# Casting the weights by DMA once per tile pair, without a bf16 copy in HBM, and a new order of work at the pair's seam

## The chip, the cores and the metric

The kernel runs on all 8 NeuronCores of one Trainium2 chip, each core on its own eighth of the tokens, with no exchange between cores. The metric is the device time of the slowest core, in microseconds (us); lower is better. The program has two states: in some executions the cores of one die, or of both, get a lower TensorE clock and the time is up to 19% longer. Such runs are called slow, and their times are left out; every comparison of times below is between fast runs. Chips also differ a little: the fast runs of the kernel before take 3500 to 3507 us on some of the chips used here and 3477 to 3482 us on others (one of them 3507), so ratios are always taken against runs of the kernel before on the same chip. The record shows where this difference is: on the slower chips, some pairs of cores have a mean clock of 0.98 in each run and take 3490 to 3506 us, while the cores at 0.99 take 3463 to 3479 us. On the other chips nearly all cores are at 0.99.

Where a profile is read, it is that of the slowest core unless another is named, because that core sets the metric.

## The reference, cut to what matters

One decoder layer over 32 x 2048 tokens, model width 1024. All sizes are those of the reference.

```python
# h   = x + RMSNorm(MixerBlock(RMSNorm(x)))
# out = h + RMSNorm(SwiGLU(RMSNorm(h)))
proj = xn @ w_in                        # 1024 -> 3840: q 512 | k 128 | v 128 | u 512 | v' 512 | gate_a 1024 | gate_b 1024
attn = banded_sink_attention(q, k, v)   # 8 heads, window 128, ALiBi, sinks
gm   = gelu(u) * (W_s LN(gelu(v')) + b) # causal 128 x 128 mixing in each chunk
merged = sigmoid(gate_a) * (attn @ w_attn_branch) + sigmoid(gate_b) * (gm @ w_gmlp_branch)
mix  = merged @ w_out
ff   = (silu(hn @ w_gate) * (hn @ w_up)) @ w_down   # 1024 -> 2816 -> 1024
```

A core has 8192 tokens: 16 tiles of 512 tokens, worked on as 8 pairs (tile A and tile B). Weights are float32 in HBM and bf16 on the chip. They are cut into 31 chunks of at most 1 MB (bf16), which stream through a ring of five buffers: `C_Q`, `C_KV`, `C_U`, `C_VG` (projections), eight `M` chunks (gates and branch projections, "merge"), two `O` (output projection), eleven `G` (gate and up) and six `D` (down). PSUM has 8 banks of 128 x 512 float32.

## The kernel before

In the kernel before, a chunk is read as float32 by a casting DMA (from GpSimd's queue) for its first few uses (one to five). It is then saved as bf16 to HBM (`wbf`) and read back from there by plain DMAs (SyncE's queue). The `M`, `O` and `D` chunks, and those of Q and KV, are streamed twice per pair, once for each tile.

```python
    def stream_init(self):
        ...                                   # M, O, G, DN: lists of chunks
        for s in range(npair):
            order += M + O + M + O + G + DN
            if s + 1 < npair:
                order += [C_Q, C_KV]
            order += DN
            if s + 1 < npair:
                order += [C_U, C_VG, C_Q, C_KV]

    def record_load(self):
        ...
        if c in self.saved:                   # bf16 copy exists: plain load
            self.dma(self.W(s, 0, ln), AP(self.wbf_d, ...), [("wbf", c)], wkey, ("W", s))
            return
        self.dma(self.W(s, 0, ln), AP(self.wsrc_d, ...), [], wkey, ("WC", s), q="pool", ...)   # cast load
        if k >= SAVE_AT[c] and c in self.order[n + 1:]:
            self.to_save.add(n)
```

Down works on one tile at a time with four PSUM banks; the projections and the attention of the next pair's tile A are laid inside the down of tile B, and x of the next tile B is loaded early in it (`k == 3`):

```python
            self.down(tA, 0)
            ...
            self.front_a(tA + 2, 0)           # Q and KV of the next tile A
            att = self.attn(tA + 2, 0)

            def hook_d(k):                    # called after each of 24 blocks of matmuls
                if k % 2 == 0:
                    next(att, None)           # a step of attention
                if k == 3:
                    self.load_x(tB + 2)
                if k in (17, 19, 21, 23):
                    bx.append(self.rms(tB + 2, (k - 17) // 2))   # normalise a 128-token block

            self.down(tB, 1, hook_d)
            ...
            self.proj_u(su, 0)
            self.tr_x(bx, 1)                  # transposes of the next tile B
            self.proj_vg(sv, 0)
            ...
```

At the start, constants are loaded and prepared before the first projection; one of the preparations is a matmul:

```python
        self.load_x(0)
        self.load_consts(0)
        self.release(0)                       # five weight loads at once
        self.load_x(1)
        self.tr_x([self.rms(0, b, ...) for b in range(NB)], 0)
        self.load_consts(1)                   # holds: self.mm(P(bk), ones, wsT, ...), needs all constants
        sq = self.acquire(C_Q)
        self.proj_q(sq, 0)
```

The softmax here doesn't subtract the row's maximum and nothing guards it: scores larger than these inputs give would overflow.

## Time and profile before

| what | value |
|---|---|
| time, median of the fast runs | 3504.9 us (fast runs 3504.12 to 3504.91, one slow run 3674.33) |
| share of TensorE busy | 95% |
| one pair of tiles, settled | 419.9 us, of which TensorE idle 9 |
| to the start of the first down | 453.2 us |
| from the start of the seventh pair's down to the end | 507.0 us |

These are lines of the profile page of the kernel before. First comes the busy time of each engine (its share, and the number of instructions). Then follow the busy share of TensorE and its granted clock in 40 equal slices, the two DMA queues (packets, MB, share of 16 engines) and the chain of waits that ended last.

```profile
PE 3332.8 (95%) x17497; PEld 1561.3 (45%) x17497; DVE 1257.0 (36%) x1817; ACT 863.0 (25%) x1199; POOL 508.6 (15%) x592
PE   2899989999999999999999999999999999999998
PEclk9888999999999999999999999999999999999999
...
q1 hardware_dynamic: 70560, 393.85, 32.7%
q0 software_dynamic: 19200, 64.75, 12.3%
...
PE 92%; DVE 3%; DMA 3%; issue 1%; POOL 1%; ACT 1%; SPq 0%; DVEq 0%; POOLq 0%; ACTq 0%
```

TensorE bounds this kernel. The row of slices shows one weak place, the start; after it there are nines, but for an 8 in the sixth slice and in the last.

The chain in order of time shows the settled period. These two lines of it (start, duration) are the transposes of the next tile A just before down, in pairs 4 and 5:

```profile
1734.32 1.79 PE ps L538 x32
...
2154.52 1.79 PE ps L538 x32
```

They are 420.2 us apart, and down begins as the transposes end (in the first pair at 451.42 + 1.79 = 453.2 us). TensorE's waits between them (in total, number, longest) are short ones:

```profile
PE ps L365 <- DVE X L371: 2.9, 1, 2.9
PE ps L365 <- DVE tmp L374: 2.8, 3, 1.1
PE ps L365 <- POOL R L371: 2.6, 2, 1.4
PE ps L365 <- DVE R L385: 0.6, 3, 0.2
PE ps L365 <- ACT tmp L368: 0.2, 1, 0.2
```

Their sum is 9.1 us. The engines' busy time in the same stretch (then clock, DMA share, GB/s) gives TensorE's work:

```profile
1734.30:2154.50 420.20, 410.88 (x2186) 193.46 (x2184) 155.92 (x225) 107.07 (x149) 56.76 (x64) 1.00 0.38 128
```

So 411 us per pair is what the matmuls take, at full clock, and a reordering can win at most 9 us there. The rest of the loss is at the edges, and the start is the largest part. This is the timeline around the first projection:

```profile
57.00 0.69 DVE L371 TENSOR_TENSOR wsT<-tmp 128x512 bf16<-128x512 f32 x1 [11.49 <-DMA g4bc<-c_g4bc]
...
57.84 0.58 PE L365 MATMUL ps<-wsT,ones 128*128 128x512 bf16 x1 [14.35 <-DVE wsT L371]
...
58.22 2.34 PE L365 MATMUL ps<-X,ring 128*128 128x512 bf16 x5
```

The first projection begins at 58.2 us. The bracket is the idle time of the engine before the instruction and what ended it.

On this core the clock is also low from 140 to 310 us: 0.81. These are the busy times of that stretch, as above, of this core and of core 5:

```profile
140.00:310.00 170.00, 166.09 (x745) 71.84 (x745) 74.01 (x101) 46.30 (x60) 52.81 (x60) 0.81 0.84 145
140.00:310.00 170.00, 161.93 (x861) 76.01 (x862) 79.35 (x107) 49.56 (x63) 54.09 (x62) 0.99 0.85 158
```

Core 5 starts 116 matmuls more; at 0.216 us each they make about 25 us. The starts of the first down agree: 423.0 us on core 4 and 426.0 on core 5, and 452 to 453 on the other six. So the low clock costs 27 to 30 us here.

### The profile page before, as it was taken

The page shows a single profiled execution, that of the slowest core. Times are in us where ns is not written, and L with a number is a line of the kernel's source. Part 1 is how long each engine was busy: PE and PEld are TensorE (multiplying, and loading weights), DVE is VectorE, ACT ScalarE, POOL GpSimd, SP SyncE. Part 2 cuts the span into 40 slices and gives each one's busy share as a digit, 9 for nine tenths or more (in the row PEclk, how much of TensorE's full clock was granted, in tenths as well). Part 3 has the DMA queues.
Part 4 walks back from the last instruction along what each step waited for, and adds up shares of the span by engine and source line. Part 5 has one row for each costly group of instructions (what it writes and reads, how often), then busy time and mean ns, then how long its engine had stood idle before and what let it go on. Part 6 is the DMA issues. An engine that isn't in the chain of part 4 may idle for free.

```text
span 3505.0 us, 46677 instructions; the slowest of 8 cores (3464.7 to 3505.0 us)
## 1 busy us (share of the span) xinstructions
PE 3332.8 (95%) x17497; PEld 1561.3 (45%) x17497; DVE 1257.0 (36%) x1817; ACT 863.0 (25%) x1199; POOL 508.6 (15%) x592
## 2 busy tenths in 40 slices
PE   2899989999999999999999999999999999999998
PEld 1444434444444444444444444444444444444443
DVE  2433125431254313542245411453125531254312
ACT  2222113321132212331132311332113321132211
POOL 1131101310012100120001300122001210012100
PEclk9888999999999999999999999999999999999999
DMA  6487688842755225432264322543235422534223
GB/s 169 67 137 154 141 164 190 162 130 83 172 184 165 85 81 190 151 133 84 82 204 139 129 83 86 187 149 120 86 129 170 145 98 82 173 123 142 84 82 135
DMA packets 89980, 461.60 MB, mean 132 GB/s; under 512 B 9632, under 2 KB 9760, under 8 KB 64032
## 3 DMA queue, kind: packets, MB, share of 16 engines
q1 hardware_dynamic: 70560, 393.85, 32.7%
q0 software_dynamic: 19200, 64.75, 12.3%
q8 instruction: 145, 2.38, 0.3%
q14 instruction: 75, 0.61, 0.1%
HBM read 460.41 MB, written 62.91 MB: 149 GB/s over the span
## 4 chain that ended last, share of the span: by engine, by line
PE 92%; DVE 3%; DMA 3%; issue 1%; POOL 1%; ACT 1%; SPq 0%; DVEq 0%; POOLq 0%; ACTq 0%
PE ps L365 90%; PE ps L538 2%; DVE tmp L374 1%; DMA tmp<-c_ident 1%; DMA wbf<-ring 1%; POOL R L371 1%; DVE X L371 1%; DMA g4bc<-c_g4bc 0%; DMA ring<-wsrc 0%; PE ps L690 0%; ACT PT L368 0%; SPq L389 0%; DVE R L385 0%; ACT tmp L368 0%; DVE xb L374 0%
## 5 line engine op out<-in xcount | busy, mean ns | idle before, releaser
L365 PE MATMUL ps<-X,ring 128*128 128x512 bf16 x8832 | 1964.7, 383 | 32.4 <-DVE X L371 23.3
L365 PEld LDWEIGHTS ps<-X,ring 128*128 128x128 bf16 x8832 | 864.5, 99 | 1081.3 <-issue 106.1
L368 ACT ACTIVATE tmp<-ps 128x1024 f32<-128x1024 f32 (+1 forms) x528 | 485.5, 921 | 2036.1 <-PE ps L365 1966.6
L365 PE MATMUL ps<-ring,R 128*128 128x512 bf16 x3840 | 859.7, 383 | 23.3 <-POOL R L371 19.8
L365 PEld LDWEIGHTS ps<-ring,R 128*128 128x128 bf16 x3840 | 372.1, 99 | 479.5 <-issue 69.7
L371 DVE TENSOR_TENSOR R<-ps,tmp 128x1024 bf16<-128x1024 f32 x176 | 215.6, 1225 | 960.9 <-PE ps L365 937.8
L371 POOL TENSOR_TENSOR stats<-stats,neghalf 128x1 f32<-128x1 f32 (+2 forms) x240 | 144.6, 602 | 1950.3 <-DVE stats L381 1710.8
L374 DVE SCALAR_TENSOR_TENSOR tmp<-tmp,ps 128x1024 f32<-128x1024 f32 x128 | 156.2, 1220 | 324.1 <-PE ps L365 315.3
L365 PE MATMUL ps<-R,ring 128*128 128x512 bf16 x1024 | 247.9, 386 | 0.0
L371 POOL TENSOR_TENSOR R<-tmp 128x512 bf16<-128x512 f32 x128 | 166.4, 1300 | 497.4 <-DVE tmp L374 465.5
L368 ACT ACTIVATE PT<-ps 128x1024 bf16<-128x1024 f32 x124 | 126.7, 1024 | 245.1 <-PE ps L365 232.7
L374 DVE SCALAR_TENSOR_TENSOR xb<-tmp,stats,xb 128x1024 f32<-128x1024 f32 x128 | 160.3, 1283 | 67.2 <-POOL stats L371 59.3
L371 DVE TENSOR_TENSOR tmp<-ps,g4bc 128x512 f32<-128x512 f32 x128 | 84.5, 688 | 268.5 <-ACT tmp L368 158.4
L365 PEld LDWEIGHTS ps<-R,ring 128*128 128x128 bf16 x1024 | 99.5, 99 | 124.8 <-issue 23.1
L371 DVE TENSOR_TENSOR X<-ps,g 128x1024 bf16<-128x1024 bf16 x128 | 150.3, 1216 | 8.8 <-PE ps L538 8.8
L371 DVE TENSOR_TENSOR PT<-PT,tbl 128x1024 bf16<-128x1024 bf16 x124 | 95.5, 771 | 151.1 <-ACT PT L368 150.3
L368 ACT ACTIVATE xn<-xb 128x1024 bf16<-128x1024 f32 x128 | 133.9, 1049 | 44.7 <-DVE stats L381 36.9
L365 PE MATMUL ps<-ring,X 128*128 128x512 bf16 (+1 forms) x1024 | 144.3, 299 | 0.0
L381 POOL TENSOR_SCALAR xn<-xb,stats 128x1024 bf16<-128x1024 f32 x124 | 138.7, 1119 | 29.7 <-POOL stats L371 25.7
L391 POOL DMA_DIRECT2D ring<-wsrc x72 | 52.9, 735 | 509.8 <-PE ps L365 416.2
L538 PE MATMUL ps<-ident,xn 128*128 128x128 bf16 x1024 | 70.2, 223 | 39.4 <-DVE stats L381 37.2
L365 PEld LDWEIGHTS ps<-ring,X 128*128 128x128 bf16 x1024 | 79.7, 98 | 62.3
(46 smaller groups left out, 897.8 us busy)
## 6 DMA issues: line engine op xcount, KB each, us to landing
ring<-wbf SPq DMA_DIRECT2D x181, 1024.0 KB, 5.0
ring<-wbf SPq DMA_DIRECT2D x125, 768.0 KB, 4.8
ring<-wsrc POOLq DMA_DIRECT2D x34, 1024.0 KB, 10.8
xb<-x SPq DMA_DIRECT2D x64, 512.0 KB, 9.4
y<-xb SPq DMA_DIRECT2D x64, 512.0 KB, 4.4
ring<-wsrc POOLq DMA_DIRECT2D x35, 768.0 KB, 10.4
wbf<-ring SPq DMA_DIRECT2D x20, 1024.0 KB, 9.2
wbf<-ring SPq DMA_DIRECT2D x10, 768.0 KB, 9.1
```

What stands on the lines that cost most here:

```text
L365: self.op("pe", lambda e: e.matmul(out, lhsT, rhs, start=start, stop=stop), reads, writes)
L368: self.op("act", lambda e: e.activation(out=out, in_=in_, func=func, **kw), reads, writes)
L371: self.op(eng, lambda e: e.tensor_tensor(out=out, in0=a, in1=b, op=alu), reads, writes)
L374: self.op("dve", lambda e: e.scalar_tensor_tensor(out=out, in0=a, scalar=sc, in1=b, op0=op0, op1=op1), reads, writes)
L381: fn = lambda e: e.tensor_scalar(out=out, in0=a, scalar1=s1, scalar2=s2, op0=op0, op1=op1)
L391: fn = lambda e: e.dma_start(out=out, in_=in_, max_dma_last_dim=max_last)
L538: self.op("pe", lambda e, o=o, x=x: e.transpose(out=o, in_=x, identity=idn), [("xn", i), ("c", "ident")], [("ps", bk)])
```

## The change

The intent: each chunk is loaded once per pair by a casting DMA, used for tile A and tile B while it is in the ring, and freed. That removes the bf16 copy and its saves, and leaves 248 weight loads in place of 390. The bytes read from HBM do not fall, since all of them are now float32. To use a down chunk for both tiles at once, down needs all 8 PSUM banks. So nothing else can run inside it, and the attention of tile A moves from down to the Q and U projections of tile B; that of tile B moves to the first merge steps. The diff, cut to its core:

```diff
     def stream_init(self):
-        ...
-        for s in range(npair):
-            order += M + O + M + O + G + DN
-            ...
+        self.order = list(range(NCH)) * (self.n_tiles // 2)

     def record_load(self, after=()):
-        if c in self.saved:
-            self.dma(self.W(s, 0, ln), AP(self.wbf_d, ...))
-            return
         self.dma(self.W(s, 0, ln), AP(self.wsrc_d, ...), list(after), [("ring", s)], ("WC", s), q="pool", ...)

-    def down(self, t, par, hook=None):
+    def down(self, tA, tB):
         for hf in range(2):
             for ci, nk in enumerate((8, 8, 6)):
                 slot = self.acquire(C_D0 + 3 * hf + ci)
+                for par in range(2):
                     for b in range(NB):
+                        bk = 4 * par + b                   # all 8 banks
                         ...
+                        if ci == 2:
+                            self.down_evac(tiles[par], par, b, hf, bk, tys[b], tj)

+    def down_evac(self, t, par, b, hf, bk, ty, tj):
+        self.act(..., AF.Square, ..., accum_out=...)       # ScalarE: sum of squares
+        self.tt("dve", yh[hf], self.P(bk), g, ALU.mult)    # VectorE: times the norm's gain
+        if hf == 0:
+            return
+        self.tt("dve", ...)                                # the two half sums
+        self.norm_stats((s, 1), EPS, rk)                   # VectorE, then GpSimd's power -1/2
+        self.stt(...)                                      # VectorE: x += y * r, waits for GpSimd
+        self.store_y(t, b)

+    def front(self, tA, tB, mid_consts=False):
+        ...                                                # Q, KV, U of A; blocks 0, 1 of B normalised
+        self.proj_vg(sv, 0, lambda h: hv(1) if h == 0 else None)   # blocks 2, 3 normalised
+        for b in range(NB):
+            self.tr_block(bx[b], 1, b, self.g1, "g1")      # transposes of B after VG of A
+        att = self.attn(tA, 0)
+        self.proj_q(sq, 1, step2)                          # Q of B, with attention of A in it
+        self.proj_u(su, 1, lambda: next(att, None))
+        ...                                                # KV of B, spatial of A, VG of B

     def record(self):
         self.load_x(0)
         self.load_consts(0)
-        self.release(0)
-        self.load_x(1)
+        self.record_load()
+        self.record_load([("xb", 0, 1)])                   # further weight loads wait for x
+        for _ in range(NSLOT - 2):
+            self.record_load([("xb", 0, 3)])
+        self.load_x(1, [("ring", 0)])
         ...
-            self.down(tA, 0)
-            self.front_a(tA + 2, 0)
-            self.down(tB, 1, hook_d)
+            self.down(tA, tB)
+            if nxt:
+                self.load_x(tB + 2)                        # x of the next B: after down
+                self.front(tA + 2, tB + 2)
```

In the same diff, merge steps of A and B alternate, and the matmul of constants moves behind the first projections (`load_consts(3)`).

## The prediction

> **What bounds it now.** TensorE: busy 95% on the page, 92% of the chain of waits that ended last. In the settled state (that chain in order of time) a pair of tiles takes 419.9 us (1734.3 to 2154.3), of which TensorE waits only 9.1 (X transposes 2.9, tmp 2.8, merged R from POOL 2.6). 608 gate/up matmuls take 131.4 us, 216 ns each. So 411 us per pair is the floor. The rest of the loss is at the edges: TensorE works 6 of the first 60 us (DMA share about 1.0; the identity landed after 29 us), the first pair reaches its last transposes at 451 us where matmuls alone need about 335, the second pair takes 444 (waits on the wbf save and weight DMAs, 15 and 27 us), the tail is 12.
>
> **What the change does.**
> - DMA: the wbf round trip goes; all 248 loads become cast loads from POOL. 64.75 MB in 12.3% of 3505 us is 150 GB/s landed, so 29.4 MB per pair takes about 196 us of 440: not a bound. A 1 MB chunk takes 7 us and feeds 13.8 us of matmuls. The Trainium skill ("DMA: Bandwidth & Descriptors", SWDGE vs HWDGE vs iDMA) says casts must be issued from GpSimd; the trace agrees (all casts are in the software queue).
> - Start: one chunk, not five, competes with the first x. Projections start at about 27 us (58 before), those last transposes come at 360 to 395, depending on whether the clock is again 0.81 from 140 to 310 us. Worth 55 to 90 us. The second pair's extra 24 us go; the tail gains 4.
> - Merge: A and B alternate, so the R waits (2.6) and the wait at gate/up (2.9) go.
> - Front, added: (a) Down's last evacuation is eight in-order VectorE blocks: 0.69 multiply, 0.26 add, 1.08 scalar to power and back, 1.22 update: 3.2 us each, while TensorE fills a bank every 1.3 us. VectorE is 17 us behind when down ends. U's first half needs bank 7, freed at +14.7, wanted at +10.4: 4 us idle. (b) x for tile B is loaded after the last of those stores; its transposes follow VG directly, with Q of B right behind. Their evacuations (4 x 1.16) queue on VectorE behind both VG tails (5.4 us each) and two normalisations. I get Q of B at +45 instead of +26. Total about 19 us idle per front. (c) Restart is cold: the Trainium skill ("TensorE: Matmul & The Clock Gate", The HAM clock gate) halves the clock after about 3.4 us idle; here 32 matmuls took 8.97 us at 92 us, not 6.9. Plus 2. (d) Denser attention: 3 to 4 us for A, 4 to 5 for B (3.6 now).
>
> **Sum.** Per pair 411 + 19 + 2 + 4 + 4, less slack: 438, against 420; seven fronts lose about 125 us. First part 379, six periods 2628, last 542: 3550 us.
>
> **What the profile should show.** TensorE busy and granted clock drop once per pair, just after down; the longest TensorE waits are on X by VectorE (about 10 us, 7 times) and tmp by VectorE (about 4). If instead Q of B starts by +30, I am wrong there and the time is near 3400. Software DMA 45 to 50% of the span, no TensorE wait on ring over 3 us in the settled state.
>
> **What would make it wrong.** VectorE chains shorter than summed; the start throttled differently; cast loads issued late by POOL's queue (closest at out-projection: 12 us in hand against about 13): slower.

## The result, and the profile after

The changed kernel takes 3612.8 us (median of four fast runs, 3609.53 to 3616.18), against 3504.9 before. The ratio is 1.0309, with a 95% interval of 1.0288 to 1.0329. A ratio here is taken over the fast runs of both kernels in the same rounds, so it is not quite the ratio of the medians that are quoted. The change makes the kernel 3.1% slower.

These are the same lines of the page as above, for the changed kernel:

```profile
PE 3325.3 (92%) x17497; PEld 1557.9 (43%) x17497; DVE 1291.2 (36%) x1977; ACT 875.2 (24%) x1206; POOL 607.8 (17%) x784
PE   4999979999799997999979999799997999979997
PEclk9999989999899998999989999899998999999999
...
q0 software_dynamic: 66432, 234.90, 39.4%
q1 hardware_dynamic: 20160, 70.08, 5.4%
...
PE 76%; DVE 9%; issue 6%; DMA 4%; POOL 2%; ACT 2%; DVEq 0%; SPq 0%; POOLq 0%; ACTq 0%
```

The start is better (the first slice is 4, not 2), but a 7 comes once per pair, and the clock dips in the same slices. On the chain that ended last, VectorE has gone from 3% to 9%. The two lines of the chain that answer to those of before are the transposes of the next tile A in pairs 4 and 5:

```profile
1716.18 1.79 PE ps L498 x32
...
2162.38 1.79 PE ps L498 x32
```

A pair now takes 446.2 us here, and 444.6 on average over six periods. In the changed kernel these transposes stand 96 matmuls (20.7 us) ahead of down, so the marks that compare are the times at which down can start: the end of the transposes, with these 20.7 us added for the changed kernel. (Its first down starts 1.6 us after this mark, after a wait.) With them, the time divides as follows.

| part | before | after | difference |
|---|---|---|---|
| to the start of the first down | 453.2 | 402.6 | -50.6 |
| six periods | 2544.8 | 2667.5 | +122.7 |
| from the seventh down to the end (one front and the tail) | 507.0 | 537.9 | +30.9 |
| span | 3505.0 | 3608.0 | +103.0 |

The busy times of a pair, for the changed kernel, show what the period is made of:

```profile
1739.00:2185.00 446.00, 415.92 (x2183) 194.75 (x2182) 159.90 (x245) 108.67 (x150) 76.31 (x97) 0.97 0.45 86
```

TensorE is busy 5.0 us longer for the same matmuls (415.9 against 410.9; the mean clock is 0.97), and idle 30.1 us, against 9.3 before. The new part, 20.8 us, is in one place, the 50 us after down, where the gaps sum to 21.1. This is TensorE's timeline there (two gaps of 0.72 and 0.26 us are cut out); down ends at 1814.5:

```profile
1814.50 8.80 PE L357 MATMUL ps<-X,ring 128*128 128x512 bf16 x40
...
1826.21 1.89 PE L357 MATMUL ps<-X,ring 128*128 128x512 bf16 x8 [1.13 <-DVE stats L363]
1829.54 5.34 PE L357 MATMUL ps<-X,ring 128*128 128x512 bf16 x24 [1.44 <-DVE stats L363]
1834.71 7.07 PE L357 MATMUL ps<-ring,X 128*128 128x512 bf16 x32
...
1846.54 1.01 PE L498 MATMUL ps<-ident,xn 128*128 128x128 bf16 x8 [4.76 <-ACT xn L360]
...
1854.47 1.01 PE L498 MATMUL ps<-ident,xn 128*128 128x128 bf16 x8 [5.18 <-POOL xn L373]
...
1864.35 3.57 PE L357 MATMUL ps<-X,ring 128*128 128x512 bf16 x8 [7.60 <-DVE X L363]
```

The last line is Q of tile B. It begins 49.9 us after the end of down (45.9 to 50.9 over the fronts), where the same matmuls without a wait would have begun at +26. The gaps are the bank waits (1.13 and 1.44), the two waits for normalised x (4.76, 5.18) and the wait for the transposed x (7.60). The eight matmuls of the last line take 3.57 us where they take 1.73 when warm: the clock from 1848 to 1864 us is 0.50. This agrees with the Trainium skill ("TensorE: Matmul & The Clock Gate", The HAM clock gate), which puts the half clock after about 3.4 us without work. Here it comes within the gap of 4.76 us: the mean clock is 1.00 up to 1844 us, 0.75 from 1844 to 1846, and 0.50 from there to 1868.

Two chains lead to this. The first is VectorE's, one block of the evacuation (A's second half), of eight:

```profile
1806.54 0.69 DVE L363 TENSOR_TENSOR tmp<-ps,g4bc 128x512 f32<-128x512 f32 x1 [28.23 <-PE ps L357]
1807.15 0.15 DVE L363 TENSOR_TENSOR stats<-stats 128x1 f32<-128x1 f32 x1
1807.41 0.15 DVE L373 TENSOR_SCALAR stats<-stats 128x1 f32<-128x1 f32 x1
1808.38 1.28 DVE L366 SCALAR_TENSOR_TENSOR xb<-tmp,stats,xb 128x1024 f32<-128x1024 f32 x1 [0.82 <-POOL stats L363]
...
1831.29 0.75 DVE L366 SCALAR_TENSOR_TENSOR xb<-tmp,stats,xb 128x512 f32<-128x512 f32 x1
```

VectorE takes 3.05 us per block (the next begins at 1809.59), TensorE fills one in 1.3. Of those, 0.82 us is VectorE standing still for GpSimd's power; it executes in order, as the Trainium skill says too ("TensorE: Matmul & The Clock Gate", Architectural detail: the array is 16× 32×32), so the next block's multiply, which could run, does not. The last update ends 17.5 us after down. The second chain hangs on its end: the last stores go out, then the load of x for tile B.

```profile
1832.53 8.11 SPq L381 DMA_DIRECT2D xb<-x  x8
1842.84 1.06 ACT L360 ACTIVATE xn<-xb 128x1024 bf16<-128x1024 f32 x1 [6.83 <-DMA xb<-x]
```

The first block of x is used 10.3 us after the load was issued (it landed after 10.2 us; over the seven fronts of this core 6.2 to 11.6, mean 8.9). Q of B follows it nearly one for one: it begins at +45.9 where the block took 6.2 us, and at +50.9 where it took 11.6. Each pair has this front once; the seventh is in the last part of the table. At the end of the program the same backlog has nothing to hide behind: the last matmul ends at 3587.2 us, this is the last update, and with its store the program ends at 3608.0:

```profile
3603.84 0.75 DVE L366 SCALAR_TENSOR_TENSOR xb<-tmp,stats,xb 128x512 f32<-128x512 f32 x1
```

The tail is 21 us; it was 12.

What remains to be shown is which of these links cost what, whether the cast traffic has a part in it, and where the 50 us at the start come from.

### The profile page after: what moved, and what is told of

Read it like the earlier page. It is cut to its first block, busy times and chain, and to the rows that moved or that the text cites. A ratio compares the mean times of both kernels' runs of the same rounds, so it can differ in the third digit from the quotient of the medians.

```text
span 3608.0 us, 46410 instructions; the slowest of 8 cores (3589.0 to 3608.0 us)
## 1 busy us (share of the span) xinstructions
PE 3325.3 (92%) x17497; PEld 1557.9 (43%) x17497; DVE 1291.2 (36%) x1977; ACT 875.2 (24%) x1206; POOL 607.8 (17%) x784
## 3 DMA queue, kind: packets, MB, share of 16 engines
q0 software_dynamic: 66432, 234.90, 39.4%
HBM read 506.28 MB, written 33.55 MB: 150 GB/s over the span
## 4 chain that ended last, share of the span: by engine, by line
PE 76%; DVE 9%; issue 6%; DMA 4%; POOL 2%; ACT 2%; DVEq 0%; SPq 0%; POOLq 0%; ACTq 0%
PE ps L357 75%; POOL stats L363 2%; DVE tmp L366 2%; DMA xb<-x 2%; DMA ring<-wsrc 1%; PE ps L498 1%; DVE tmp L363 1%; ACT PT L360 1%; DVE bnst L576 1%; DVE X L363 1%; DVE xb L366 1%; DVE R L373 1%; DMA lnbpp<-c_lnbpp 0%; DVE PT L363 0%; DVE stats L373 0%
## 5 line engine op out<-in xcount | busy, mean ns | idle before, releaser
L357 PE MATMUL ps<-ring,R 128*128 128x512 bf16 x3840 | 833.5, 379 | 7.8 <-DMA ring<-wsrc 6.2
L357 PEld LDWEIGHTS ps<-ring,R 128*128 128x128 bf16 x3840 | 375.0, 98 | 460.4 <-issue 10.6
L383 POOL DMA_DIRECT2D ring<-wsrc x248 | 181.5, 732 | 1587.2 <-PE ps L357 1553.9
L363 POOL TENSOR_TENSOR stats<-stats,neghalf 128x1 f32<-128x1 f32 (+1 forms) x288 | 163.7, 568 | 871.0 <-DVE stats L373 742.3
L363 DVE TENSOR_TENSOR tmp<-ps,g4bc 128x512 f32<-128x512 f32 x96 | 66.0, 687 | 469.8 <-ACT tmp L360 271.3
L363 POOL TENSOR_TENSOR R<-tmp 128x512 bf16<-128x512 f32 x112 | 141.4, 1262 | 510.5 <-DVE tmp L366 483.3
L498 PE MATMUL ps<-ident,xn 128*128 128x128 bf16 x1024 | 83.0, 238 | 106.2 <-POOL xn L373 61.7
L366 DVE SCALAR_TENSOR_TENSOR xb<-tmp,stats,xb 128x1024 f32<-128x1024 f32 (+1 forms) x128 | 147.4, 1151 | 73.8 <-POOL stats L363 63.0
L363 DVE TENSOR_TENSOR X<-ps,g 128x1024 bf16<-128x1024 bf16 x128 | 150.7, 1217 | 20.7 <-PE ps L498 20.4
L498 PEld LDWEIGHTS ps<-ident,xn 128*128 128x128 bf16 x1024 | 71.0, 106 | 128.2 <-issue 115.0
L373 POOL TENSOR_SCALAR xn<-xb,stats 128x1024 bf16<-128x1024 f32 x108 | 120.7, 1117 | 25.9 <-POOL stats L363 23.7
L363 DVE TENSOR_TENSOR PT<-PT,tbl 128x1024 bf16<-128x1024 bf16 x124 | 85.6, 701 | 108.7 <-ACT PT L360 108.3
## 6 DMA issues: line engine op xcount, KB each, us to landing
xb<-x SPq DMA_DIRECT2D x64, 512.0 KB, 11.3
```

The lines of the kernel that those rows point to most:

```text
L357: self.op("pe", lambda e: e.matmul(out, lhsT, rhs, start=start, stop=stop), reads, writes)
L363: self.op(eng, lambda e: e.tensor_tensor(out=out, in0=a, in1=b, op=alu), reads, writes)
L366: self.op("dve", lambda e: e.scalar_tensor_tensor(out=out, in0=a, scalar=sc, in1=b, op0=op0, op1=op1), reads, writes)
L373: fn = lambda e: e.tensor_scalar(out=out, in0=a, scalar1=s1, scalar2=s2, op0=op0, op1=op1)
L383: fn = lambda e: e.dma_start(out=out, in_=in_, max_dma_last_dim=max_last)
L498: self.op("pe", lambda e, o=o, x=x: e.transpose(out=o, in_=x, identity=idn), [("xn", i), ("c", "ident")], [("ps", bk)])
```

## The experiments

Sixteen kernels ran, all with correct results. "Q of B" is the start of that projection after the end of down, the number read above as +49.9. Ratios are to the kernel before, in fast runs of the same rounds. The period is the mean of six. It and Q of B are those of the slowest core of the profiled run, but for e4 (core 4) and e5 (core 6), where that core's clock was low for a time.

| run | what is different | fast runs, us | ratio [95%] | period | Q of B |
|---|---|---|---|---|---|
| changed kernel | | 3609.5 to 3616.2 | 1.0309 [1.0288, 1.0329] | 444.6 | +45.9 to +50.9 |
| e1_bf16copy | bf16 copy kept | 3600.5, 3602.4 | 1.0277 [1.0256, 1.0297] | 442.2 | +45 to +48 |
| e2_xearly | x of B loaded earlier | 3570.3, 3572.4 | 1.0191 [1.0170, 1.0211] | 438.3 | +42 to +43 |
| e3_pipe | update deferred by a block | 3566.6, 3571.3 | 1.0184 [1.0164, 1.0204] | 438.8 | +42 to +44 |
| e4_order | e2, and B's transposes before VG of A | 3507.5 to 3553.8 | 1.0012 [0.9996, 1.0029] | 431.1 | +35 to +37 |
| e5_all | e4 and e3 | 3460.7 to 3463.8 | 0.9887 [0.9870, 0.9903] | 422.3 | +27.3 to +28.3 |
| e6_attn | B's attention on 4 merge steps | 3614.5 to 3617.3 | 1.0325 [1.0310, 1.0340] | 445.6 | +45 to +50 |
| e7_all_bf16 | e5 and e1 | 3447.4 to 3453.7 | 0.9857 [0.9840, 0.9873] | 423.4 | +27.4 to +31.4 |
| e8_best | e5, e6 and new start | 3458.9, 3461.2 | 0.9881 [0.9861, 0.9901] | 427.2 | +27.4 to +33.7 |
| e9_start | e5 and new start | 3456.4 to 3462.6 | 0.9948 [0.9932, 0.9964] | 426.9 | +27.4 to +32.7 |
| e10_spread | e9, A's attention spread | 3519.1, 3527.3 | none given | 433.4 | +27.4 to +33.6 |
| e11_spread_bf16 | e10 and e1 | 3511.6, 3511.9 | 1.0096 [1.0074, 1.0118] | 430.8 | +27.4 to +29.8 |
| e12_before_start | kernel before, new load order | 3476.7 to 3481.8 | 1.0001 [0.9985, 1.0017] | | |
| e13_before_consts | e12, constants moved too | 3468.0, 3470.1 | 0.9975 [0.9951, 0.9999] | | |
| e14_best2 | e5, new start and e1 | 3444.7 to 3450.3 | 0.9918 [0.9895, 0.9942] | 423.4 | +27.4 to +30.6 |
| e15_xlater | next A's x out of the burst | 3609.4, 3609.7 | 1.0350 [1.0268, 1.0431] | 444.0 | +45.3 to +49.3 |
| e16_best_xlater | e14 and e15 | 3443.3 to 3443.9 | 0.9874 [0.9796, 0.9952] | 423.0 | +27.3 to +30.9 |

The runs e9 to e16 were on chips where the kernel before takes about 3480 us; for those the times tell more than the ratios when they are compared with e1 to e8 (kernel before 3501 to 3504 us in the median). Two of e4's six fast runs, 3533.7 (the profiled one) and 3553.8 us, had a lower clock on two cores for a time; the other four take 3507.5 to 3510.6.

### e1: is it the cast traffic?

My theory was that VectorE's evacuation and the late x cause the loss. The rival was the cast loads: software DMA is busy 39.4% of the span, up from 12.3%. This run takes away most of the casts and leaves the order of work.

```diff
+        if n >= NCH:                                 # from pair 2 on: plain bf16 load
+            self.dma(self.W(s, 0, ln), AP(self.wbf_d, ...), [("wbf", c)], [("ring", s)], ("WC", s), q="pool", ...)
+            return
     def acquire(self, expect):
+        if n < NCH:                                  # pair 1: save each chunk
+            self.dma(AP(self.wbf_d, ...), self.W(s, 0, ln), [("ring", s)], [("wbf", expect)], ("WS", s))
```

> The changed kernel, but from the second pair on its weights come from a bf16 copy in HBM (saved during the first pair), by the same issues on POOL in the same order: half the bytes read, no cast. Main theory (the loss is VectorE's in-order queue around the front of each pair): the period from one pair's last transposes to the next stays at 440 to 446 us (444.6 in the changed kernel), total 3590 to 3620, apart from what the saves cost in the first pair. At most 3 us per pair may come from a faster landing of x, which shares the DMA engines with one cast load. Rival (the loss is the cast traffic: late weights, x starved behind cast loads): period 430 or less, total below 3540.

Measured: 1.0277, 11 us less than the changed kernel by the fast times; the period falls from 444.6 to 442.2, and Q of B starts 1.6 us sooner in the mean (+46.8 against +48.4). The cast traffic is not the cause of the loss. What it costs is about 2 us per front, as a neighbour of x's load.

### e2, e3, e4: the three links, one at a time

e2 asks for x of tile B right after the first of B's updates, not after the last store:

```diff
+        if par == 1 and b == 0 and t + 2 < self.n_tiles:
+            self.load_x(t + 2)
...
             if nxt:
-                self.load_x(tB + 2)
                 self.front(tA + 2, tB + 2)
```

> The changed kernel, but x for tile B of the next pair is loaded as soon as tile A's four stores are issued, not after tile B's. Main theory: the ScalarE squares no longer wait for x (8 us of wait per front now), but VectorE's backlog and the order (transposes behind both VG tails) stay; Q of B starts 43 to 45 us after down's end instead of 50, period about 438 to 440, total 3565 to 3580. Rival (x landing alone is the loss): Q of B by 30, period 425, total below 3480. Rival (weights by cast DMA): nothing changes, 3605 to 3620.

Measured: 1.0191, period 438.3, so 6.3 us per front, as expected. The late issue of this load is worth that much of the 24 us by which Q of B is late in the front shown. The wait for the transposed x stays as it was (62.4 us in all, longest 7.8).

e3 puts the update of a block behind the multiply of the next one, so that VectorE has work while GpSimd computes the power:

```diff
+        def update():
             self.stt(self.xblk(t, b), self.T(ty), self.ST(s), self.xblk(t, b), ALU.mult, ALU.add, ...)
             self.store_y(t, b)
+        if self.late is not None:
+            self.late()
+        self.late = update
```

> The changed kernel, but in down's last evacuation the update of a block is issued on VectorE after the next block's multiply, add and scaling, so that the trip to POOL for the power is hidden: 2.3 us a block in place of 3.1. Main theory: VectorE's backlog at down's end falls from 17.5 to about 12 us, U no longer waits for banks 6 and 7 (2.6 us), x is loaded 5 to 6 us sooner, Q of B starts at 43 to 45 us instead of 50; period 437 to 440, and the tail of the program shrinks from 21 to about 15 us; total 3555 to 3575. Rival (cast DMA): nothing but the tail changes, 3600 to 3615.

Measured, as expected: 1.0184, period 438.8, tail 15 us in place of 21 (last matmul 3550.4, end 3565.0). The backlog's end moves the x load and with it the whole front.

e4 is e2 with all four normalisations ahead of U, and the transposes between U and VG, where the kernel before had them:

```diff
+        bx = [self.rms(tB, b, "pool" if b % 2 == 0 else "dve") for b in range(NB)]
         self.proj_u(su, 0)
-        hv(0)
-        self.proj_vg(sv, 0, lambda h: hv(1) if h == 0 else None)
+        for b in range(NB):
+            self.tr_block(bx[b], 1, b, self.g1, "g1")
+        self.proj_vg(sv, 0)
-        for b in range(NB):
-            self.tr_block(bx[b], 1, b, self.g1, "g1")
```

> As with the early x, and also the old order of the front: normalisations of tile B ahead of U, its transposes between U and VG, so that VG's 6.9 us of matmuls cover their evacuation and they stand ahead of VG's tails on VectorE. The backlog of down stays. Main theory: Q of B starts about 33 us after down's end (early x alone 44, changed kernel 50, no idle 26), period 427 to 430, total 3485 to 3510. If the early x alone gives as much as this, the order of the transposes is not a cause.

Measured: 1.0012, period 431.1 (1 us over the expected range), 7.2 us below e2. The wait of Q of B for the transposed x is gone. Among TensorE's waits over the run, these two lines show it, first of the changed kernel:

```profile
PE ps L357 <- DVE X L363: 62.3, 9, 7.6
```

and of e4:

```profile
PE ps L357 <- DVE X L363: 1.5, 1, 1.5
```

### e5: do the three add up?

> Early x, the old order of the front, and the shorter evacuation of down together (all else as in the changed kernel). Main theory: the backlog at down's end is about 12 us, x is there, the transposes go between U and VG: Q of B starts 28 to 30 us after down's end (36 with the old order but the long backlog, 50 in the changed kernel, 26 with no idle), period 421 to 425, tail about 15 us, total 3425 to 3455, so about 2% below the kernel before. If it stays above 3490, something other than the front holds the changed kernel back.

Measured: 0.9887. The profile fell in a slow run; on its core 6, in the periods with a full clock, the period is 422.3 and Q of B starts at +27.3 to +28.3, in effect without a wait. The start of Q of B and the period fall together: from the changed kernel's slowest core to this one, Q of B by 20.8 us in the mean (48.4 to 27.6), the period by 22.3 (444.6 to 422.3). So the front accounts for nearly the whole loss of the period.

The time is 6 us above the expected range at its nearest, and the cores show why. In the run of 3460.67 us four cores take 3436 to 3441 us, inside the range, and the other four 3456 to 3459. e9, which has the same fronts and a profile in a fast run, shows the same split (3435 to 3442 and 3459 to 3460 us). There the cores of the slower half begin Q of B at up to +34, because blocks of x land late, and those of the faster half at +27.3 in most fronts. The slowest core sets the time.

What keeps the period from falling below that of the kernel before is another thing: the waits inside attention have grown. These are TensorE's waits on exponentials of the attention in the changed kernel and in e5 (core 6; e14, profiled in a fast run, has 29.5, 26, 3.1):

```profile
PE ps L357 <- DVE PT L363: 15.1, 22, 2.1
```

```profile
PE ps L358 <- DVE PT L364: 30.0, 27, 3.0
```

Part of that is new in each front: at the first step of A's attention TensorE waits 3.1 us for the first product of exponentials and table, where it waited 0.5 us in the order of the changed kernel (e15's timeline). In VectorE's timeline of e14, which has the same order of work, the layer norm of VG stands straight ahead of that product (the list is cut to three lines):

```profile
1772.94 0.17 DVE L373 TENSOR_SCALAR stats<-stats 128x2 f32<-128x2 f32 x1
1774.05 1.00 DVE L375 TENSOR_SCALAR R<-tmp,stats 128x512 bf16<-128x512 f32 x2 [0.95 <-POOL stats L365]
1774.97 1.29 DVE L365 TENSOR_TENSOR PT<-PT,tbl 128x1024 bf16<-128x1024 bf16 x2
```

VectorE takes VG's layer norm first, because it executes in order, and the attention follows. The settled period is thus back where the kernel before has it (420), not below.

### e6, e8, e10, e11: trying to take the attention's waits away

e6 gives one step of B's attention to each of four merge steps, in place of two to each of three:

```diff
         self.feat_r(slot, 2048, br, par, 0)
-        if inter is not None:
-            next(inter, None)
         self.feat_r(slot, 2560, br + 1, par, 4)
...
-            for c in range(3):
+            for c in range(4):
                 mA(c, att)
```

> The changed kernel, but tile B's attention is spread over four merge steps of tile A (three parts a step) instead of three (four parts a step). Main theory: denser attention costs little, about 5 us of TensorE waits per pair in B's part; spreading takes off half of it: total 15 to 25 us lower, 3588 to 3600. Rival (the attention riding on the merge steps is a main part of the loss): at least 60 us lower.

A miss: 1.0325, no gain. The waits on the exponentials fell from 15.1 to 4.9 us, but the waits on the merge's own products rose. The line for these in the changed kernel, and in e6:

```profile
PE ps L357 <- DVE tmp L366: 12.5, 16, 1.2
```

```profile
PE ps L357 <- DVE tmp L366: 31.3, 24, 3.3
```

e8 was e5 with e6's spreading and a new start (constants first, normalisations before transposes):

```diff
-        self.load_x(0)
         self.load_consts(0)
+        self.load_x(0)
...
+        bx = [self.rms(0, b, "pool" if b % 2 == 0 else "dve") for b in range(NB)]
         for b in range(NB):
-            self.tr_block(self.rms(0, b, "dve"), 0, b, self.g1, "g1")
+            self.tr_block(bx[b], 0, b, self.g1, "g1")
```

> The three mends, attention of B over four merge steps, and a start that loads the constants ahead of x and issues all four normalisations ahead of the transposes. Expected: first projection at about 30 us instead of 39, period about 419 to 422, total 3400 to 3425, 2.3% to 3% below the kernel before.

Missed by 34 us: 0.9881, the same as e5. The cores differ as in e5 (3434.6 us on core 0, where Q of B starts at +27.4, 3459.7 on core 5, where it starts at +31 to +34 in five of the seven fronts, because two of the four blocks of x land late).

e10 gives A's attention half its density in Q of B, and puts VG of B ahead of KV of B:

```diff
-        self.proj_q(sq, 1, step2)
+        self.proj_q(sq, 1, lambda: next(att, None))
-        self.proj_u(su, 1, lambda: next(att, None))
+        self.proj_u(su, 1, step2)
+        self.proj_vg(sv, 1)
         self.proj_kv(sk, 1, tB)
-        self.spatial(0)
-        self.proj_vg(sv, 1)
```

> As the last one, and tile A's attention starts at half the density in Q (one part per eight matmuls instead of two, two in U instead of one), so that VG's tail on VectorE is over before its first product is wanted; VG of B is computed before KV of B, so that KV covers VG's tail before tile B's attention. Expected: the 3 us wait for PT right after the front goes (8 times), about 1 us per pair in B's part: period 417 to 419, total 3420 to 3435. If PT's wait only moves into U, the total stays at 3455 or above.

A miss in the other direction: 3519.1 us, about 60 more than e9. The wait was not removed but moved, to one on VectorE's copy of Q in the same place:

```profile
1819.42 3.30 PE L358 MATMUL ps<-X,ring 128*128 128x512 bf16 x8 [3.63 <-DVE R L378]
```

and over the run the waits on that copy came to 28.9 us and those on the merge's products to 30.5. The run changes two things at once, the density and the place of VG, so which of them costs the 60 us was not separated. e11 is e10 with the bf16 copy:

> The same with weights from a bf16 copy in HBM from the second pair on. The three mends gained 0.3% from this copy. Main theory: within 0.4% of the run before it (at most 15 us lower), from x landing sooner, not from weights: TensorE's waits on ring stay under 10 us in all in both.

It was 1.0096, so the same loss. In e6 and in e10 a wait that was taken away in one step came back in another, as long or longer. An order that lowers their sum was not found.

### e7: the bf16 copy on top of the mends

> The run with all three mends, and from the second pair on its weights come from a bf16 copy in HBM. Main theory: the cast traffic costs nothing once x is early: within 0.5% of the run with the three mends, period within 2 us of it. Rival (the cast loads cost time that the front's idle had hidden): period 5 us or more shorter, total 35 us or more lower.

Measured: 0.9857, against 0.9887 for e5: 0.3% (7 to 16 us by the fast times). The median landing of a 1 MB chunk is 5.1 us here, against 8.5 us for the casts in e5. So the traffic has a price once the chains are mended, but a small one, and the removal of the copy, which was the point of the change, is a cost and not a gain. The cores tell where the price is paid: the fastest core of a run is no faster with the copy (3432 to 3437 us, and 3432 to 3441 in e5), the slowest is (3447 to 3454, and 3461 to 3464). So what the copy gives is on the cores where x lands late.

### e9, e12, e13: what is the new start worth, and why?

> The three mends of the front and the new start (constants first, normalisations ahead of the transposes), attention as in the changed kernel. The run that had this start and attention over four merge steps was no faster than the three mends alone, and spreading the attention alone cost 3 us. Expected: first projection at 34 to 35 us, 4 to 6 us below the three mends: 3455 to 3460.

e9 (e5 with the new start) is at 3456.4 to 3462.6 us, 2 us below e5, although the first projection comes at 34.6 us in place of 39.3. On half the cores x of tile B lands late in the fronts, which takes the rest.

e12 puts the load order of the changed kernel (one weight chunk first, the others behind x; the identity, not shown, ahead of the other constants) into the kernel before. The prediction had named that order as the reason for the better start.

```diff
         self.load_x(0)
         self.load_consts(0)
-        self.release(0)
-        self.load_x(1)
+        self.record_load()
+        self.record_load([("xb", 0, 1)])
+        for _ in range(NSLOT - 2):
+            self.record_load([("xb", 0, 3)])
+        self.load_x(1, [("ring", 0)])
```

> The kernel before with one part of the change alone: at the start only one weight chunk competes with the first x (the second waits for the second block of x, the other three for the fourth), x of the second tile waits for the first chunk, and the identity is loaded first. Main theory: the changed kernel's gain is in the start: first projection at 35 to 45 us instead of 58, and the first pair's last transposes come 15 to 25 us sooner than 451, or 45 to 60 if the 0.81 clock between 140 and 310 us goes as well, which it did in the changed kernel. Total 3480 to 3490, or about 3450 without the low clock. Rival: nothing outside 3495 to 3510, as the loads themselves end no sooner.

It is worth nothing: 1.0001. The first transposes end at 31 us, but the first projection still stands behind the matmul of constants:

```profile
60.29 0.59 PE L365 MATMUL ps<-wsT,ones 128*128 128x512 bf16 x1 [28.49 <-DVE wsT L371]
```

So e13 moves that matmul as well, as the changed kernel does, with the changed kernel's order and place of the constants' loads (cut here).

```diff
         self.proj_kv(sk, 0, 0)
+        self.load_consts(2)                    # the exponential of the bias table
         for _ in self.attn(0, 0): pass
         ...
         self.proj_vg(sv, 1)
+        self.load_consts(3)                    # wsT and its matmul
         self.spatial(0)
```

> The kernel before, with the start of the changed kernel complete: the new order of loads and the matmul of the constants (wsT x ones) moved out of TensorE's way, behind the first projection's blocks. Theory: it is this matmul, which waits until 59 us for the last constant, that costs the start, not the load order (the order alone gave 1.0001). Then the first projection begins near 35 us in place of 60, the first pair's last transposes come near 410 us in place of 431.5, and the total is 20 to 25 us below the kernel before of the same rounds (ratio 0.993 to 0.995). Rival: another wait for constants (tbl, a weight chunk) takes its place and the ratio is 0.998 or more.

The theory is half right. The first projection begins at 34.3 us, as expected. But the ratio is 0.9975, about 9 us, and not 20 to 25. Another wait took the place of the first one: in the kernel before, attention of A comes right behind KV of A with nothing beside it, and needs the bias table, which is a constant too:

```profile
60.78 0.60 PE L365 MATMUL ps<-vtok,PT 128*128 128x65 bf16 x8 [13.12 <-ACT PT L368]
...
123.86 0.59 PE L365 MATMUL ps<-wsT,ones 128*128 128x512 bf16 x1 [6.70 <-DVE wsT L371]
```

The first pair's last transposes come at 416.4 us, 15 us ahead of e12 (431.5), and 8 of those are given back by the seventh pair (2960.0 against 2966.6 us). So the gain of the changed kernel at the start is not one of the order of loads. By its timeline it comes from the order of work: after KV of A stand U, VG and the transposes of B, which need no constant, and attention comes after them; no run tests that part alone. How much is it? Cores 4 and 5 of the kernel before, with the clock at 1.00 and 0.99 from 140 to 310 us, start the first down at 423.0 and 426.0 us, against 453.2 on the core of the table. So of the 50.6 us in the table, 27 to 30 are the low clock that the kernel before had on that core, and 20 to 23 are the order. e12, where that clock is 0.96, lies between (433.3 us). Why the changed kernel has the full clock there (1.00 on all eight cores) stays open; in e5's slow run, cores 0, 1, 4 and 5 have 0.81 in the same stretch.

### e14: the best of it

e14 is e5 with the new start and the bf16 copy.

> The changed kernel with the three mends (early load of x, transposes of tile B between U and VG, update of a block after the next block's multiply), the new start, and a bf16 copy of the weights saved in pair 1. Theory: the terms add; the start's gain sits in the first 400 us and the copy's gain (0.3% between the run with all three mends and the same with the copy) in pairs 2 to 8. So about 0.983 to 0.988 of the kernel before. Rival: the copy's gain came from the loads of x alone and is gone once those land in time, then 0.989 to 0.995 as without the copy.

It takes 3444.7 to 3450.3 us, 0.9918 of the kernel before on that chip: short of the expected ratio. By the same marks as above, and against e12's profile (which is as fast as the kernel before), the first down can start at 391.4 us against 433.3, six periods take 2540 against 2535, and the last part 511.5 against 506.8. So 42 us are won in the first pair, and the 17 us by which e12's second pair is longer than a settled one (12.9 of them in one wait behind a bf16 save) are gone too. The settled pairs give some of it back: 422.7 us on average, and 419.6 before. One pair of e14, by busy times:

```profile
1642.70:2065.10 422.40, 411.43 (x2186) 193.40 (x2183) 159.90 (x245) 108.44 (x150) 75.87 (x97) 1.00 0.26 90
```

TensorE's own work is back at 411.4 us and at full clock; the idle time is 11.0, against 9.3 before.

### e15, e16: what makes x land late?

In the front of the changed kernel, eight loads of x leave in one burst: tile B's four and, behind them, the four of the tile A after it. e15 holds the second four back until the first merge step is done.

```diff
-            if nxt:
-                self.load_x(tA + 2)
             att = self.attn(tB, 1)
 ...
             for c in range(3):
                 mA(c, att)
+            if nxt:
+                self.load_x(tA + 2, kR(0, 12))
```

> The changed kernel, where only the load of the next pair's first tile (the other half of the burst of eight 512 KB loads of x after down) waits until the first merge step is done. Theory: the first block of tile B's x takes 10.3 us because both tiles, 4 MB, go out together beside a cast load; with half the burst gone it lands after 6 us or less, Q of B begins at about +45 to +46 after the end of down in place of +49 to +50, a pair takes 440 to 442 us in place of 444.6, and the total is 20 to 30 us below the changed kernel, ratio 1.022 to 1.026. Rival: the landing is long for the cast load or the stores beside it, not for the other tile; then the ratio stays at 1.029 to 1.032 and Q of B at +48 or later.

The theory fails, and the rival is nearer. Two fast runs, 3609.4 and 3609.7 us, are 3 us below the changed kernel's median, the period is 444.0 us on the slowest core, and Q of B begins at +47.3 in the mean, 1 us sooner. (The ratio of 1.035 is taken on a chip whose kernel before takes 3480 us and has a wide interval, so the times are compared here.) In the front that answers to the one shown, the first block of x is used 9.0 us after its issue, not 10.3:

```profile
1831.37 2.56 SPq L381 DMA_DIRECT2D xb<-x  x4
...
1840.35 1.06 ACT L360 ACTIVATE xn<-xb 128x1024 bf16<-128x1024 f32 x1 [5.52 <-DMA xb<-x]
```

Over the seven fronts the landing of that block takes 7.8 us in the mean, against 8.9 in the changed kernel and 7.4 in e1. So the other tile's x is worth about 1 us of it, and the casts about 1.5. What makes up the rest was not separated. The four blocks of the tile itself (2 MB) are in flight together, with two stores and a weight chunk, and the second block is used only 1.3 us after the first. The changed kernel's trace shows how full the engines are there: stores issued from 1815 to 1823 us land in 2.6 us (median), but the one issued at 1828.8, behind a casting load that itself takes 11.6 us, needs 10.6, and the DMA share is 0.85 to 1.07 in each 2 us from 1832 to 1842.

> The best version so far (three mends, new start, bf16 copy) with the same deferral. Theory: on half of its cores tile B's later blocks of x still land late (Q of B at +29 to +32 in place of +27.4), because the other tile's load is in the same burst; deferred, all fronts begin Q of B at +27.4 to +28, a pair gains 1 to 2 us and the ratio to the kernel before falls by 0.002 to 0.004, to about 0.988 to 0.990. Rival: x is out of the way already since it is asked for early; ratio 0.991 to 0.993, unchanged.

e16 is the same deferral in the best version: 3443.3, 3443.5 and 3443.9 us in three fast runs. Against the fast runs of the kernel before (3477 to 3482, and one of 3507.26 that is counted as fast and makes the interval wide) that is 0.9874 [0.9796, 0.9952]; against their median, 3481.06, it is 0.989. It is the fastest version found, but 1 us ahead of e14's fastest run. The fronts of the best version still start Q of B at +27.3 to +31, so this burst was not the cause of the spread between cores either.

## Why the prediction was right or wrong

The direction was right, but the size was not: the sum, 3550 us, was a loss of 1.3%, and the loss is 3.1% (3612.8 us). The mechanism held: the loss is in the front after down, by VectorE's backlog and the late x. What failed is the size of three terms of the sum: the landing of x in the front, the cold clock ("Plus 2") and the tail ("gains 4").

- **The floor and the bound: right.** "411 us per pair is the floor" was read from the waits; the busy time of a pair is 410.9.
- **The front: right in kind, too small.** "I get Q of B at +45 instead of +26": it came at +45.9 to +50.9, +49.9 in the front shown. In the mean of the seven fronts it is +48.4, 3.4 us late. The idle time itself, "about 19 us", came out at 21.1. The term that was mis-sized is the landing of x. The trace shows 10.2 in the front shown and 8.9 in the mean; by the step from +45.9 to +50.9 between landings of 6.2 and 11.6 us, "+45" answers to about 5 us (an estimate). The page of the kernel before already had the number that should have been used: a median of 9.4 us for the 512 KB loads of x. The Trainium skill ("DMA: Bandwidth & Descriptors", Anatomy of one DMA) has a fit for one DMA that GpSimd issues, 2.0 us plus bytes over 436e3, from which 3.2 us for 512 KB can be estimated; x is issued by SyncE and lands among other loads, so that estimate was no guide here. The same page (Issuing engines are not separate DMA queues) says that the DMAs of all engines run on the same 16 and interleave, and the trace agrees: x shares them with stores, a cast load and its own three other blocks. Asking for x earlier (e2) is worth 6.3 us per front.
- **The cold clock: too small.** "Plus 2": TensorE's busy time per pair rose by 5.0 us. There are three gaps of over 4 us in this front, and the clock stays at 0.50 from 1846 to 1868 us, through the second and the third of them, not only for the matmuls of the restart.
- **The bank wait: right in kind.** "4 us idle" measured as 1.13 + 1.44 = 2.6. "VectorE is 17 us behind when down ends" measured as 17.5.
- **The attention: right enough.** 3 to 4 us forecast for A and 4 to 5 for B; about 2.5 and 5.3 measured.
- **The tail: wrong.** "the tail gains 4" overlooked that VectorE's backlog, which the front hides in part, is bare at the end. 21 us, not 8: 13 us of error.
- **The start: right by luck.** 379 us to the first pair's last transposes forecast, 380.1 measured. But the first projection came at 39.3 us and not at "about 27", and the text's reason ("one chunk, not five, competes with the first x") is refuted by e12. e13 shows that the constants' matmul is a part of it; that the order of work after it is the rest is argued from the timeline. That the clock was full from 140 to 310 us, worth 27 to 30 us, made up for the late projection; the text had left that clock open.
- **The DMA: right.** "not a bound": 39.4% of the span (45 to 50% was forecast), TensorE waits 6.2 us in all on weight chunks, at most 1.7 at once, and without the casts the loss stays (e1).
- **The sum.** 379 + 6 x 438 + 542 forecast, 380 + 6 x 444.6 + 560 measured: 40 us in the periods and 18 in the last part. The three terms account for these 58, by estimate: 3.4 us (Q of B later than forecast) and 3.0 (5.0 of clock, not 2) in each of seven fronts make 45, and the tail 13. e2's 6.3 us per front is not this error: it also removes the part of the wait that had been forecast.

What the predicted signs showed: the drop of busy time and clock once per pair, just after down, is there. "the longest TensorE waits are on X by VectorE (about 10 us, 7 times)" measured as 7.6; but as long in sum is the wait for normalised x from GpSimd, ScalarE and VectorE (which the text has in its chain, but not in its list), while the "about 4" on tmp was 1.2 at most.

Why did the expected gain of the change, one load per chunk and no copy, bring nothing in the settled state? It could not: there the kernel before waits 9 us per pair, none of it for a weight. The traffic that was removed was already hidden, and the price was the hiding place: down of one tile at a time with four banks was where tile A's projections and attention, and tile B's x and its evacuation, overlapped with matmuls. With all 8 banks in down, that work is exposed at the seam. With the three mends it is hidden again. Against the kernel before on its chip, e5 is 1.1% faster, all of it from the first two pairs; but 27 to 30 of these 39 us are the low clock that the kernel before has on that kind of chip. Where it has not, e9 gains 0.5%, and with the bf16 copy e14 gains 0.8% and e16 about 1.1%.

## What to carry to other kernels

Before a transfer is removed, look at whether anything waits for it: here, in the settled pairs, nothing did, and the change paid for it with the one stretch in which slow evacuations overlapped with matmuls. When a loop is restructured so that an in-order engine gets its work in a burst, cost the burst's whole chain (each instruction, the round trip to another engine, then the loads that hang on its end) with the landing times that the trace shows under load, and cost it a second time at the end of the program, where nothing hides it. If the chain is exposed, first ask for the next data earlier, then put independent work into the round trip, then move the consumer's producer ahead of long work: the three together were worth 4.2% of the time here, the first and the third 3.0% of it.

## What the Trainium skill lacked or had wrong

- "DMA: Bandwidth & Descriptors" says that DMAs interleave, but has no landing time for loads that share the engines. Here the first 512 KB of x took 6.2 to 11.6 us in the fronts, and the median over the run was 11.3 us (9.4 in the kernel before). Its fit for one DMA (Anatomy of one DMA) is for those that GpSimd issues; it has none for SyncE's.
- The same page says that casts are issued from GpSimd only (SWDGE vs HWDGE vs iDMA), which agrees, but has no rate for them. Here the casting queue landed 234.9 MB in 39.4% of 3608 us, which is 165 GB/s of bf16; the same bytes took 22.3% of the span in e1, where all but the first pair's come from a bf16 copy, and a 1 MB chunk landed in 5.1 us (e7) against 8.5 us (e5).
- "TensorE: Matmul & The Clock Gate" says that a die goes to 13/16 of the clock within about 5 to 20 us of a third core's dense matmuls, and stays there while the load lasts. In the kernel before, six cores ran at 0.81 from 140 to 310 us, and cores 4 and 5 at 1.00 and 0.99, though cores 6 and 7 of the same die were among the six. From 1000 to 3000 us all eight cores were dense, at 1.00. So here the limit neither held for a whole die nor as long as the load lasted. The slow runs look more like the page: in one of 4132.28 us (kernel before, in the rounds of e15) cores 4 to 7 have a mean clock of 0.81.
- No page that I found gives the cost of a scalar's round trip from VectorE to GpSimd and back. In the trace it is about 1.0 us from VectorE's instruction to its next one, of which 0.55 is GpSimd's and 0.82 is VectorE standing still.
